# Moving the transposes of the gated activation to the border between the float32r and the bf16 products of gate/up

## The chip, the cores and the metric

The kernel runs on one core of a Trainium2 chip. The metric is the device time of one execution in microseconds. Five engines work side by side, each through its own list of instructions in order: TensorE (PE; PEld is its loading of weights), VectorE (DVE), ScalarE (ACT), GpSimd (POOL) and SyncE (SP), which issues most transfers. They hand work to each other by semaphores.

## The reference

One encoder block over 1024 tokens of width 1024: RMSNorm, one projection to q, k and v, differential attention beside dilated window attention, an output projection with a residual, RMSNorm, sixteen experts that each choose 128 tokens, a residual, and a final RMSNorm. The change lies in the experts:

```python
def expert_choice_ffn(h, w_router, w_gate, w_up, w_down):
    cap = EC_K * S // N_EXPERTS            # 128 tokens per expert
    aff = jax.nn.softmax((h @ w_router).astype(jnp.float32), axis=-1)
    g, idx = lax.top_k(aff.transpose(0, 2, 1), cap)
    ...
    def run_expert(args):
        wg, wu, wd, ie, ge = args
        xe = h[b_rows, ie]
        he = jax.nn.silu(xe @ wg) * (xe @ wu)
        return (he @ wd) * ge[..., None].astype(h.dtype)
```

## The kernel before, in words

An expert's hidden width of 2816 is worked in 11 slices of 256 columns. One slice of one expert is a **unit**; there are 16 x 11 = 176 of them, and the loop over them (L1487 to L1501) is where the kernel spends two thirds of its time.

Each float32 matrix is split in two. ScalarE writes the high part `wh` as float32r (L1324), VectorE subtracts it and writes the rest `wl` as bf16 (L1326). The text calls the first a **split** and the second a **subtraction**; each takes half a piece of weights (128 x 1024 numbers). A unit has three pieces: two of gate/up, one of down, so six splits and six subtractions. Of the activations there are a high part `xh` and a low part `xl`, both float32r.

For a unit i TensorE runs, in `gate_up`, sixteen float32r products with `wh` (L1354 with `xh`, L1355 with `xl`, by turns, k = 0 to 7) and then eight bf16 products with `wl` (L1363). ScalarE makes `sg`, the silu of the gate half (L1368), and VectorE multiplies it by the up half (L1369, the **gating product**). TensorE must turn `sg` before it can meet the down weights. That is done one unit late, in the middle of the products of unit i + 1: `middle` is called there, it emits the splits of the down weights of unit i, and `turn_gated` emits two transposes (L1375) and the splitting of their output into `eh` on ScalarE (L1381) and `el` on VectorE (L1382). Behind the bf16 products of unit i + 1 come the down products of unit i (`down`): four bf16 ones of `wl` with `eh` (L1392), then eight float32r ones, four with `eh` (L1395) and four with `el` (L1396). `sg`, `eh` and `el` have one buffer each.

The order on ScalarE and VectorE of all splits, subtractions, `sg`, `eh`, `el` and the gating product is the order in which the code emits them: `in_turn` ties each to the one before. On ScalarE a unit reads: eh, three splits, sg, three splits; the last two of these six are for the down weights. The scheduler of the tile framework places everything else, by its own costs. That holds for three things that come once per expert:

- **the end**: behind an expert's last down product ScalarE copies the output times its gate (ROW, L1454, two halves) and GpSimd adds it to the result in memory;
- **the pick**: in the unit behind s = 3 VectorE makes a one-hot matrix (L1226), TensorE takes eight small products with it (P, L1232), and VectorE reduces their output to token numbers and gates (L1234 to L1238), with which GpSimd fetches the next expert's rows;
- **the turned rows**: behind the unit of s = 8 TensorE turns these rows with eight transposes (L1297), and ScalarE and VectorE split them into the next `xh` and `xl` (L96).

`issue_behind(a, b)` only orders a behind b on their engine; it waits for nothing. In `gate_up` it ties the first product of k = 3 behind the last transpose (L1359), so the transposes stand after k = TG = 2. While the first expert runs, a search for the sixteen thresholds (L1174 to L1186) shares VectorE with it.

Of the kernel before, what the change touches and what calls it, by code (L numbers as in the profile page):

```python
# [49 lines left out]
PK, PT = 3, 8  # L50
PK0, PT0 = 6, 9
SB, XB = 1, 2
TG = 2
OHN = lambda e: 8
HIB, LOB = 8, 10
STQ = lambda t: 2
# [26 lines left out]
def tile_hybrid_encoder_block(ctx, tc, x, norm1_g, w_in, lam_v, subln_g, w_out, rel_bias, hot,  # L83
# [14 lines left out]
    def issue_behind(later, earlier):  # L98

        tc.add_manual_dep(later.ins, earlier.ins.name,  # L100
                          mybir.DependencyInfo(mybir.DependencyClass.NoSync, mybir.DependencyReason.DATA),
                          reason="issue_behind")
# [56 lines left out]
    def top(t):  # L159

        n = len(t.shape) - 1
        return t.bitcast(BF)[(slice(None),) * n + (slice(1, None, 2),)]
# [1142 lines left out]
    def in_turn(ins):  # L1305

        eng = str(ins.ins.engine)
        if eng in tails:
            issue_behind(ins, tails[eng])
        tails[eng] = ins  # L1310
        return ins
# [36 lines left out]
    def gate_up(xt, wt, middle):  # L1348
        _, _, xh, xl = xt
        pg = ps_g.tile([128, 2, FS], F32, name="pg")  # L1350
        cut = lambda k: [v(k % 4 * 512, 512) for v in wt[k // 4]]
        for k in range(KD):
            wh = cut(k)[0]
            hh = nc.tensor.matmul(pg, xh[:, k, :], wh, start=(k == 0), stop=False)  # L1354
            mm_ = nc.tensor.matmul(pg, xl[:, k, :], wh, start=False, stop=False)  # L1355
            if k == TG:
                last_mm[0] = mm_
                middle()
            if k == TG + 1 and turned_g:  # L1359
                issue_behind(hh, turned_g.pop())  # L1360

        for k in range(KD):
            low = nc.tensor.matmul(pg, top(xh)[:, k, :], cut(k)[1], start=False, stop=(k == KD - 1))  # L1363
            if k == 0:
                issue_behind(low, mm_)
        last_mm[0] = low
        sg = sm.tile([128, FS], F32, name="sg", bufs=SB)
        in_turn(nc.scalar.activation(sg, pg[:, 0, :], AF.Silu))  # L1368
        in_turn(nc.vector.tensor_mul(sg, sg, pg[:, 1, :]))  # L1369
        return sg  # L1370
# [88 lines left out]
    last_mm, last_hi, turned_g = [None], [None], []  # L1459
# [17 lines left out]
    def middle(i):  # L1477
        next(later, None)
        if i >= 0:
            split_piece(i, 2)  # L1480
            sgs[i] = turn_gated(sgs[i])
        if i + 2 < len(units):
            split_piece(i + 2, 0)
            if (i + 2, 1) not in split:
                split_half(i + 2, 1, 0)

    for i, (e, s) in enumerate(units):  # L1487
        load_pieces()
        wt = [parts(i, 0), parts(i, 1)]
        sgs[i] = gate_up(prep[e], wt, lambda: middle(i - 1))  # L1490
        if i + 1 < len(units):
            split_piece(i + 1, 1)
        next(later, None)
        if s == (PK if e else PK0) and e + 1 < n_experts:
            prep[e + 1] = pick(e + 1, slot_all[0][:, :, e + 1:e + 2])
        if s == (PT if e else PT0) and e + 1 < n_experts:
            prep[e + 1] = turn3(*prep[e + 1], after=last_mm[0])
        if i > 0:
            close(i - 1)
        if done_p[0] == len(pieces) and last is None and (s > 1 or n_experts == 1):  # L1500
            last = final_load()  # L1501
# [82 lines left out]
```

## Time and profile before

| | us |
|---|---|
| median of three runs | 2269.86 (2263.57 to 2271.57) |
| profiled execution | 2268.57 |
| its span | 2266.8 |
| TensorE busy | 2168.2 (96%) |
| VectorE busy | 1891.6 (83%) |
| ScalarE busy | 1600.3 (71%) |

The span runs from the first to the last instruction; the time of the execution has 1.8 us more around it. Busy times overlap, since the engines work side by side. In the chain of work that ended last TensorE has 84% of the span, VectorE 6%, transfers 5%. By lines, TensorE's products of gate/up (L1354, L1355, L1363) make 41% of it.

### The profile page before, as it was taken

What the parts mean: (1) busy time and instruction counts of PE and PEld (TensorE: products, weight loads), DVE (VectorE), ACT (ScalarE), POOL (GpSimd) and SP (SyncE); (2) the same over time, 40 slices, a digit from 0 to 9 for tenths busy, and PEclk for the clock granted to TensorE, in tenths of its full rate; (3) what the DMA queues carried; (4) which work ended last, traced back from release to release, by engine and by line L of the source; (5) the groups of instructions that cost most, each with busy time, mean ns of one, the idle gap of its engine ahead of it and who ended that gap; (6) DMA issues with size and microseconds to landing.
All of it is one profiled execution on the core that took longest, in us unless ns stands there. A gap on an engine that the chain in (4) does not pass through costs nothing.

```text
span 2266.8 us, 31806 instructions
## 1 busy us (share of the span) xinstructions
PE 2168.2 (96%) x11051; PEld 1604.7 (71%) x11171; DVE 1891.6 (83%) x2874; ACT 1600.3 (71%) x2431; POOL 223.6 (10%) x264
## 2 busy tenths in 40 slices
PE   8999998989996999999999999999999999999995
PEld 7899897767774666676666666666667667666663
DVE  5466774677877999999899999999999999999996
ACT  5576773556743677777777777787777777777785
POOL 1000100345533000000000000000000000000000
PEclk9999999999997999999999999999999999999998
DMA  5767656588568799999999999999999999999983
GB/s 185 233 179 209 182 164 171 154 200 224 177 232 267 275 360 392 374 385 390 367 401 374 377 386 375 406 373 377 388 371 397 374 390 385 374 388 381 388 344 129
DMA packets 172749, 708.25 MB, mean 312 GB/s; under 512 B 19690, under 2 KB 54634, under 8 KB 106658
## 3 DMA queue, kind: packets, MB, share of 16 engines
q1 hardware_dynamic: 160452, 670.46, 80.2%
q0 software_dynamic: 7184, 25.69, 4.0%
q10 hardware_dynamic: 4952, 10.05, 1.3%
q8 instruction: 88, 1.44, 0.3%
q14 instruction: 73, 0.60, 0.1%
HBM read 649.89 MB, written 57.75 MB: 312 GB/s over the span
## 4 chain that ended last, share of the span: by engine, by line
PE 84%; DVE 6%; DMA 5%; issue 2%; ACT 2%; SPq 0%; POOL 0%; POOLq 0%; ACTq 0%; DVEq 0%
PE pg L1354 14%; PE pg L1355 14%; PE pg L1363 13%; PE pm L154 10%; PE py L1396 7%; PE py L1395 7%; PE py L1392 6%; PE av L154 4%; PE ps L154 3%; PE pt L157 3%; PE px L1375 2%; PE py L154 1%; DVE wl L1326 1%; DMA xt<-xa_d 1%; DMA w<-q_d 1%
## 5 line engine op out<-in xcount | busy, mean ns | idle before, releaser
L1326 DVE TENSOR_TENSOR wl<-w,wh 128x1024 bf16<-128x1024 f32 (+1 forms) x1062 | 1237.9, 1217 | 74.9 <-ACT wh L1324 71.5
L1324 ACT ACTIVATE wh<-w 128x1024 fp32r<-128x1024 f32 (+1 forms) x1070 | 1041.6, 1041 | 8.9 <-DVE up L1088 5.4
L1354 PE MATMUL pg<-wh,xh 128*128 128x512 f32 x1408 | 570.7, 405 | 0.0
L1355 PE MATMUL pg<-wh,xl 128*128 128x512 f32 x1408 | 553.9, 393 | 1.3 <-DVE xl L96 1.3
L1363 PE MATMUL pg<-wl,xh 128*128 128x512 bf16 x1313 | 316.5, 380 | 6.3
L1395 PE MATMUL py<-wh,eh 128*128 128x512 f32 x704 | 310.7, 441 | 0.0
L1354 PEld LDWEIGHTS pg<-wh,xh 128*128 128x128 f32 x1408 | 265.5, 189 | 56.5 <-issue 2.1
L1355 PEld LDWEIGHTS pg<-wh,xl 128*128 128x128 f32 x1408 | 266.1, 189 | 53.9 <-DVE xl L96 2.0
L1396 PE MATMUL py<-wh,el 128*128 128x512 f32 x704 | 278.3, 395 | 0.0
L1363 PEld LDWEIGHTS <-xh 128*128 128x128 bf16 x1408 | 123.6, 98 | 170.0 <-issue 45.0
L1381 ACT ACTIVATE eh<-px 128x256 fp32r<-128x256 f32 x176 | 67.5, 384 | 166.0 <-PE px L1375 166.0
L1392 PE MATMUL py<-wl,eh 128*128 128x512 bf16 x701 | 180.4, 379 | 1.0 <-ACT eh L1381 0.9
L1368 ACT ACTIVATE sg<-pg 128x256 f32<-128x256 f32 x176 | 67.5, 384 | 137.6 <-PE pg L1363 137.6
L1395 PEld LDWEIGHTS py<-wh,eh 128*128 128x128 f32 x704 | 132.5, 188 | 44.3
L1396 PEld LDWEIGHTS py<-wh,el 128*128 128x128 f32 x704 | 132.5, 188 | 28.7 <-issue 0.4
L154 PE MATMUL pm<-hT,wh 128*128 128x512 f32 x464 | 146.6, 396 | 0.1
L1392 PEld LDWEIGHTS <-eh 128*128 128x128 bf16 x704 | 68.8, 98 | 80.4 <-ACT eh L1381 1.2
L1455 POOL DMA_INDIRECT x_d<-row,idx x15 | 24.1, 1607 | 933.7 <-ACT row L1454 870.3
L154 PE MATMUL pm<-wh,hT 128*128 128x256 f32 x512 | 102.4, 290 | 0.1
L154 PEld LDWEIGHTS pm<-hT,wh 128*128 128x128 f32 x464 | 83.9, 188 | 15.8 <-DVE ee L361 0.5
L418 ACT ACTIVATE e<-e,nm 128x1024 f32<-128x1024 f32 x64 | 73.5, 1148 | 29.3 <-DVE nm L416 22.8
L96 DVE TENSOR_TENSOR pl<-pt,ph 128x512 fp32r<-128x512 f32 x96 | 65.3, 684 | 33.0 <-ACT ph L96 33.0
(303 smaller groups left out, 2884.4 us busy)
## 6 DMA issues: line engine op xcount, KB each, us to landing
w<-in_w_moe_dram SPq DMA_DIRECT2D x514, 1024.0 KB, 7.3
w<-in_w_moe_dram SPq DMA_DIRECT2D x56, 256.0 KB, 4.2
wraw<-in_w_in_dram SPq DMA_DIRECT2D x48, 256.0 KB, 4.1
v_d<-ee SPq DMA_DIRECT2D x16, 512.0 KB, 4.0
q_d<-ee SPq DMA_DIRECT2D x16, 512.0 KB, 3.8
k_d<-ee SPq DMA_DIRECT2D x16, 512.0 KB, 3.4
k<-k_d SPq DMA_DIRECT2D x16, 512.0 KB, 6.0
xt<-in_x_dram SPq DMA_DIRECT2D x8, 512.0 KB, 6.9
```

Source lines behind the costliest of these rows:

```text
L154: return pin(nc.tensor.matmul(*args, **kw))
L157: return pin(nc.tensor.transpose(*args, **kw))
L418: nc.scalar.activation(e, e, AF.Exp, bias=nm, scale=-1.0, accum_out=l)
L1324: hi = nc.scalar.activation(wh[:, cs], src, AF.Copy)
L1326: sub = eng.tensor_sub(wl[:, cs], src, r32(wh)[:, cs])
L1354: hh = nc.tensor.matmul(pg, xh[:, k, :], wh, start=(k == 0), stop=False)
L1355: mm_ = nc.tensor.matmul(pg, xl[:, k, :], wh, start=False, stop=False)
L1363: low = nc.tensor.matmul(pg, top(xh)[:, k, :], cut(k)[1], start=False, stop=(k == KD - 1))
L1368: in_turn(nc.scalar.activation(sg, pg[:, 0, :], AF.Silu))
L1392: low.append(lambda j=j, c=c, ns=ns, n=n: nc.tensor.matmul(py[:, ns], top(eh)[:, j, :], wl(c, 512), start=(s == 0 and j == 0), stop=False))
L1395: nc.tensor.matmul(py[:, ns], eh[:, j, :], wh(c, 512), start=False, stop=False),
L1396: nc.tensor.matmul(py[:, ns], el[:, j, :], wh(c, 512), start=False, stop=(s == NS - 1 and j == 1))))
```

## The change

`TG` becomes 7. So `middle` is called behind the last float32r product of a unit instead of behind that of k = 2, and the transposes are ordered behind that product. The order that tied the product of k = 3 behind the transposes goes, and the first bf16 product is tied behind them instead.

```diff
-TG = 2
+TG = 7
 ...
             if k == TG:
                 last_mm[0] = mm_
                 middle()
-            if k == TG + 1 and turned_g:
-                issue_behind(hh, turned_g.pop())
 
         for k in range(KD):
             low = nc.tensor.matmul(pg, top(xh)[:, k, :], cut(k)[1], start=False, stop=(k == KD - 1))
             if k == 0:
                 issue_behind(low, mm_)
+                if turned_g:
+                    issue_behind(low, turned_g.pop())
         last_mm[0] = low
```

Two lines go in `gate_up`, so its bf16 products are on L1361 in the changed file; the other lines spoken of keep their numbers. The instructions are the same ones. Their order changes at four places.

On TensorE, in an ordinary unit, the transposes of `sg` (px<-ident,sg) stood between float32r products before:

```order
L1354 MATMUL pg<-wh,xh 128x512
L1355 MATMUL pg<-wh,xl 128x512
L1375 MATMUL px<-ident,sg 128x128 x2
L1354 MATMUL pg<-wh,xh 128x512
L1355 MATMUL pg<-wh,xl 128x512
```

and now:

```order
L1354 MATMUL pg<-wh,xh 128x512
L1355 MATMUL pg<-wh,xl 128x512
L1375 MATMUL px<-ident,sg 128x128 x2
L1361 LDWEIGHTS xh
L1361 MATMUL pg<-wl,xh 128x512
```

They moved past ten float32r products, to right ahead of the eight bf16 ones.

On TensorE, at the pick, the last of the eight products with the one-hot matrix `oh` stood ahead of the last float32r product:

```order
L1232 LDWEIGHTS oh
L1232 MATMUL pr<-aux,oh 128x5
L1355 MATMUL pg<-wh,xl 128x512
L1363 LDWEIGHTS xh
L1363 MATMUL pg<-wl,xh 128x512
```

and now, for eleven of the experts (py is the down output of the expert at work):

```order
L1232 LDWEIGHTS oh
L1232 MATMUL pr<-aux,oh 128x5
L1361 LDWEIGHTS xh
L1361 MATMUL pg<-wl,xh 128x512
L1392 LDWEIGHTS eh
L1392 MATMUL py_19250<-wl,eh 128x512
L1392 LDWEIGHTS eh
L1392 MATMUL py_19250<-wl,eh 128x512
L1354 MATMUL pg<-wh,xh 128x512
L1392 LDWEIGHTS eh
L1392 MATMUL py_19250<-wl,eh 128x512
```

The eight small products moved behind the seventh bf16 product, and one float32r product of the next unit stands among the down products. VectorE's own order at this place is unchanged: gating product, subtraction, one-hot, subtraction, the three reductions, subtraction, el.

On ScalarE, at the end of an expert, the two ROW copies (row<-py) stood together behind the fourth split:

```order
L1381 ACTIVATE eh<-px 128x256
L1324 ACTIVATE wh<-w 128x1024 x3
L1368 ACTIVATE sg<-pg 128x256
L1324 ACTIVATE wh<-w 128x1024
L1454 ACTIVATE row<-py_18363,gate 128x512 x2
L1324 ACTIVATE wh<-w 128x1024 x2
L1381 ACTIVATE eh<-px 128x256
```

and now, for twelve of fifteen experts:

```order
L1381 ACTIVATE eh<-px 128x256
L1324 ACTIVATE wh<-w 128x1024 x2
L1454 ACTIVATE row<-py_18363,gate 128x512
L1324 ACTIVATE wh<-w 128x1024
L1368 ACTIVATE sg<-pg 128x256
L1324 ACTIVATE wh<-w 128x1024
L1454 ACTIVATE row<-py_18363,gate 128x512
L1324 ACTIVATE wh<-w 128x1024 x2
L1381 ACTIVATE eh<-px 128x256
```

The first copy moved ahead of a split and of sg. For the first three experts both copies now stand behind the fifth split, where they stood behind the sixth. The fourth place, where rows are turned, changes likewise for eleven experts: TensorE's eight transposes are parted into four ahead of the bf16 down products and four behind them, and the copies on ScalarE and VectorE stand apart, the first right behind eh and el, the second behind two splits.

## Rows read from the trace of the kernel before

**Rows 1.** Windows: stretch, its us, busy us (count) per engine, granted clock, DMA share, GB/s.
```profile
743.00:803.00 60.00, 53.72 (x245) 35.04 (x249) 59.94 (x118) 38.77 (x49) 0.00 (x0) 1.00 0.87 307
1300.00:1400.00 100.00, 99.60 (x460) 69.10 (x465) 92.55 (x101) 77.66 (x99) 2.83 (x2) 1.00 0.98 387
```

**Rows 2.** Timeline of TensorE, an ordinary unit: start us, duration us, engine, line, operation, xcount.
```profile
1601.25 0.40 PE L1354 MATMUL pg<-wh,xh 128*128 128x512 f32 x1
...
1602.64 0.38 PE L1375 MATMUL px<-ident,sg 128*128 128x128 f32 x2
...
1603.09 0.39 PE L1355 MATMUL pg<-wh,xl 128*128 128x512 f32 x1
...
1604.93 0.39 PE L1355 MATMUL pg<-wh,xl 128*128 128x512 f32 x1
1605.39 1.67 PE L1363 MATMUL pg<-wl,xh 128*128 128x512 bf16 x7
1606.90 1.03 PE L1392 MATMUL py<-wl,eh 128*128 128x512 bf16 x4
...
1609.63 0.40 PE L1354 MATMUL pg<-wh,xh 128*128 128x512 f32 x1
```

**Rows 3.** Timeline of TensorE where an expert's rows are turned.
```profile
1559.90 0.38 PE L1375 MATMUL px<-ident,sg 128*128 128x128 f32 x2
...
1564.16 1.04 PE L1297 MATMUL px<-ident,row 128*128 128x128 f32 x8
1565.03 1.03 PE L1392 MATMUL py<-wl,eh 128*128 128x512 bf16 x4
1569.15 0.38 PE L1375 MATMUL px<-ident,sg 128*128 128x128 f32 x2
```

**Rows 4.** Timeline of ScalarE, the same place.
```profile
1560.32 0.38 ACT L1381 ACTIVATE eh<-px 128x256 fp32r<-128x256 f32 x1 [1.10 <-PE px L1375]
1560.60 2.00 ACT L1324 ACTIVATE wh<-w 128x1024 fp32r<-128x1024 f32 x2
1564.80 1.08 ACT L96 ACTIVATE xh<-px 128x512 fp32r<-128x512 f32 x2 [2.20 <-PE px L1297]
```

**Rows 5.** Timeline of VectorE, the same place.
```profile
1560.76 0.42 DVE L1382 TENSOR_TENSOR el<-px,eh 128x256 fp32r<-128x256 f32 x1
1561.68 2.36 DVE L1326 TENSOR_TENSOR wl<-w,wh 128x1024 bf16<-128x1024 f32 x2 [0.49 <-ACT wh L1324]
1565.43 1.29 DVE L96 TENSOR_TENSOR xl<-px,xh 128x512 fp32r<-128x512 f32 x2 [1.39 <-ACT xh L96]
...
1571.74 0.42 DVE L1382 TENSOR_TENSOR el<-px,eh 128x256 fp32r<-128x256 f32 x1
```

**Rows 6.** Timeline of TensorE at a pick.
```profile
1526.13 0.38 PE L1375 MATMUL px<-ident,sg 128*128 128x128 f32 x2
...
1528.42 0.36 PE L1232 MATMUL pr<-aux,oh 128*128 128x5 bf16 x8
```

**Rows 7.** Timeline of VectorE at the same pick.
```profile
1528.82 0.16 DVE L1234 TENSOR_REDUCE num<-pr 128x1 f32<-128x2 f32 x1 [1.74 <-PE pr L1232]
...
1529.08 1.22 DVE L1326 TENSOR_TENSOR wl<-w,wh 128x1024 bf16<-128x1024 f32 x1
1530.21 0.42 DVE L1382 TENSOR_TENSOR el<-px,eh 128x256 fp32r<-128x256 f32 x1
```

**Rows 8.** Timeline of TensorE: an expert's last down product.
```profile
1499.39 0.40 PE L1396 MATMUL py<-wh,el 128*128 128x512 f32 x1
```

**Rows 9.** Timeline of ScalarE at the same end of an expert.
```profile
1499.82 1.27 ACT L1454 ACTIVATE row<-py,gate 128x512 f32<-128x512 f32 x2 [1.40 <-PE py L1396]
1500.98 2.01 ACT L1324 ACTIVATE wh<-w 128x1024 fp32r<-128x1024 f32 x2
1502.87 0.38 ACT L1381 ACTIVATE eh<-px 128x256 fp32r<-128x256 f32 x1
```

**Rows 10.** Timeline of VectorE at the same end of an expert.
```profile
1504.34 0.42 DVE L1382 TENSOR_TENSOR el<-px,eh 128x256 fp32r<-128x256 f32 x1
```

## The prediction

> **What bounds the kernel now.** I read the windows of the trace first, then one ordinary unit of the experts on TensorE, and then the three places in an expert where something other than the ordinary unit happens. The windows show where the limit is: of 100 us among the experts TensorE is busy 99.60, VectorE 92.55, ScalarE 77.66, at a granted clock of 1.00 [rows 1]. So TensorE sets the pace, and VectorE has only some 7% to spare. In the unit's timeline the reader is to see that products follow each other with no hole: 8.38 us from the first product of one unit (1601.25) to that of the next (1609.63) [rows 2]. A float32r product takes 0.230 (eight from 1603.09 to 1604.93), a bf16 one 0.216 (seven from 1605.39 to 1606.90), and from the start of the transposes to the second product behind them 0.45 pass, so the pair costs 0.22 in its old place [rows 2].
>
> **A clock for one unit.** Let t = 0 be the start of the two transposes, with the number of the unit whose gated activation they turn left out. ScalarE's eh starts at 0.42 and its next split at 0.70 [rows 3, 4]; el starts on VectorE at 0.86 and its first subtraction at 1.78, because that one waits for ScalarE's split, which stands 1.08 before it [rows 3 to 5]. From then on a subtraction follows each 1.13 (1529.08 to 1530.21) [rows 7], a split on ScalarE each 0.945 (two from 1500.98 to 1502.87) [rows 9]; el and the gating product take 0.34 (their 0.42 less the 0.09 by which a subtraction's 1.22 overlaps the next). VectorE's order is el, three subtractions, the gating product, three subtractions, el; the last two of these six, call them D1 and D2, make the low halves of the down weights that TensorE's bf16 down products read. Thus D2 starts at 1.78 + 3 x 1.13 + 0.34 + 2 x 1.13 = 7.77 and is done at 8.99.
>
> **What the change takes away.** The transposes leave the float32r products and stand before the bf16 ones. Four transposes and a bf16 product in a row are seen already, where an expert's rows are turned: eight transposes from 1564.16, the bf16 product at 1565.03, so 0.109 each and nothing added at the end [rows 3]; a pair costs 0.218. The old switch from float32r to bf16 takes 0.46 for two products (1604.93 to 1605.39) where 0.230 + 0.216 = 0.446 would do [rows 2]. The gain is about 0.016 a unit, 175 units, 3 us. Its bounds are nothing and 0.03 a unit, 5 us. The Trainium skill ("TensorE: Matmul & The Clock Gate", section "Step-by-step: what each phase is for") says that TensorE pulls a weight load ahead of running products, so that the order of kinds would not matter; by that rule the 3 us fall away and the sum below ends 3 us higher; the row's 0.46 against 0.446 says that it is nearly so.
>
> **What it moves.** Ten float32r products now run before the transposes instead of after them: eh and el come 10 x 0.230 = 2.30 us later, and TensorE's demand for them does not. Behind the transposes stand eight bf16 products (0.22 + 1.73 = 1.95), then the down products: the first two want eh and D1 at 1.95, the next two want D2 at 2.38, and the first product with el comes at 3.04. The unit ends at 4.68, the next transposes start at 8.36. Before, the same demands were 2.30 later: D2 at 4.68. In an ordinary unit D2 is done at 8.99 and wanted at 8.36 + 2.38 = 10.74: the slack falls from 4.05 to 1.75 us, and nothing waits. The deadline of the gating product, which the transposes read, becomes 2.30 us looser in exchange. So the question is which places make VectorE or ScalarE lose more than 1.75 us against TensorE. The trace has three of them per expert, visible as el's lateness, beyond 0.86, behind its transposes: at the end of an expert 3.34 - 0.86 = 2.48 (el at 1504.34; the transposes six products behind the last product of 1499.39, at 1501.00) [rows 8, 10]; where the next expert's tokens are picked 4.08 - 0.86 = 3.22 [rows 6, 7]; where its rows are turned 2.59 - 0.86 = 1.73 [rows 3, 5]. All three were covered by 4.05. Less 1.75 they leave 0.73 + 1.47 + 0 = 2.2 us per expert. Since phases and orders shift, I work each one out anew.
>
> **End of an expert.** The last product's output is read by two ROW copies on ScalarE (L1454), which start 0.43 behind that product's start and take 0.58 each [rows 8, 9]. In the new order the first stands earlier, behind only two splits, so ScalarE, free at 2.59, is held until 4.45 + 0.43 = 4.88; queued behind it are a split, sg, a split, the second ROW, D1's and D2's splits and eh. They start at 5.46, 6.40, 6.67, 7.61, 8.19, 9.14 and 10.08. VectorE follows: subtraction 6.54, gating product 7.67, subtraction 8.01, D1 9.27, D2 10.40, done at 11.62. TensorE wants D2 at 10.74: it waits about 0.9. Twelve experts have this order (the first three put the copies behind five splits, which costs nothing): 10.8 us.
>
> **The pick.** VectorE's reduction num waits for eight small products (P, L1232) and starts 0.40 behind the first of them, D2 another 0.26 later [rows 6, 7]. P stood between float32r products; now it stands before the eighth bf16 product, at 8.36 + 0.22 + 7 x 0.216 = 10.09. So num comes at 10.49, D2 at 10.75, done at 11.97. TensorE has left only P (up to 0.3), one bf16 product, two down products and one early float32r product of the next unit (0.22 + 0.43 + 0.23) and would want D2 at 11.27: it waits 0.7, eleven times, 7.7 us.
>
> **The turned rows.** The eight transposes are split in two fours, the second behind the down products. ScalarE's first copy starts 0.64 behind the first transpose (1564.80) and VectorE's 0.63 behind that [rows 3 to 5]: 2.59 and 3.22. Two splits, a copy, a split, sg and three splits follow, on VectorE 4.18, 5.31, copy 6.44, 7.05, gating 8.18, 8.52, D1 9.65, D2 10.78, done 12.00. The next transposes come at 9.24, so D2 is wanted at 11.62: 0.4, eleven times, 4.4 us. In the ordinary unit behind each place VectorE gains some 0.3 to 0.9 back and D2 is in time.
>
> **The start.** From 743 to 803 us the first expert shares VectorE with the search for the threshold, and VectorE is busy 59.94 of 60 [rows 1]. It does the same work in a slightly other order, so I take 0. Bounds: TensorE's 6 us of idleness there are the most that could be won, and 0.86 of waiting for el in seven units, 6 us, could be lost.
>
> **The sum.** 10.8 + 7.7 + 4.4 - 3 = 20 us on the profiled execution's 2268.57 (span 2266.8; 1.3 below the median of three, 2269.86): 2289. The waits are not in the trace of before; their ends are 0 (slack enough) and the whole lateness with no slack, 12 x 2.48 + 11 x (3.22 + 1.73) = 84 us. I stay near the subtraction of the slack, since its terms all have rows: 2.2 by the old lateness, 2.0 by the new schedule.
>
> **Rivals.**
> - The slack holds (0.14). If hand-overs are 0.5 us quicker than I took them or ROW's wait ends earlier, only the gain is left: 2268.57 - 3 = 2266, not slower. For it speaks that the other 140 units have 1.75 to spare; against it that two of three old latenesses exceed that. It decides at 1.75 us.
> - One or two of the three places stall (0.12): the pick alone gives 2273, pick and end 2284; I call it 2277. The pick's chain is the tightest, as P itself is late.
> - The start decides (0.04). TensorE idles 6 us of 60 there [rows 1], waiting for VectorE. Were the transposes the thing that waits, moving them back would win up to 6, and if the later stalls also fail, 2260. VectorE's 59.94 speaks against it.
> - It grows (0.08). A stall leaves a lateness that meets the next place, or the granted clock falls. From 743 to 803 TensorE was busy 53.72 of 60 and was still granted 1.00 [rows 1]. The skill (same page, "A second HAM failure mode: psum-queue depth-cycling") tells of short idle times between products that make the clock go up and down; no such fall is in that row. The price, one stall in eight followed by a unit at half clock: 4 x 8.4 = 34 more, 2323; by lateness alone 12 x 0.9 more, 2300. I take 2310.
>
> **How the numbers follow.** My forecast has 0.62 and, alone, spans 2279 to 2300 (each stall 0.3 us less or more: 34 x 0.3 = 10). The range for 8 in 10 takes in the partial case below and part of the growth above: 2270 to 2303. About 0.5%, 11 us, is what a measurement of this kernel can tell from no change. Slower, above 2281: most of my forecast (0.59), the growth (0.08), a little of the partial case (0.03), 0.70. Within: 0.26. Faster, below 2258.5: 0.04.
>
> **What would show it.** Right: a unit without a special place at 8.36, transposes followed at 0.22 by a bf16 product; ROW waiting some 2.3 us on ScalarE; a wait of TensorE for L1326 before the third down product (L1392), 34 times, 0.4 to 0.9 each; idle time of VectorE before el in ordinary units. Wrong: TensorE still at 99.6 of 100 among the experts, or waits for another releaser (eh, the gating product), or a granted clock below 1.00 there.

## The result, and the profile after

The changed kernel takes 2280.10 us (median of five executions, 2278.15 to 2281.28); the kernel before, run beside it, 2267.09 (2263.57 to 2271.57). The ratio is 1.0055, with a 95% interval from 1.0044 to 1.0067: slower by some 13 us, or half a percent.

The windows answer to [rows 1] (same stretches, same columns):

```profile
743.00:803.00 60.00, 55.16 (x279) 37.26 (x278) 58.90 (x117) 39.87 (x51) 0.00 (x0) 1.00 0.92 325
1300.00:1400.00 100.00, 98.68 (x460) 70.01 (x459) 91.15 (x100) 75.20 (x97) 3.36 (x2) 1.00 0.97 374
```

Among the experts TensorE fell from 99.60 to 98.68 of 100, at the same granted clock of 1.00, the upper level (2.4 GHz). It now waits. (The 0.40 that was missing from 100 before are no waits: that trace lacks the record of the first bf16 product in many units, which is why [rows 2] shows x7. So TensorE was hardly ever idle.) The view of what TensorE's products waited for, from 1000 us to 2200 us (total us, times, longest), was empty before and now has one line:

```profile
PE py L1392 <- DVE wl L1326: 14.9, 34, 0.7
```

The bf16 down products wait for a subtraction, 34 times: 12 ends of an expert, 11 picks, 11 turned rows. The loading of weights (PEld) waits too, for a split, 24 times, twice at each of the 12 ends:

```profile
PEld pg L1354 <- ACT wh L1324: 9.1, 24, 0.5
```

**An ordinary unit.** TensorE's timeline, which answers to [rows 2]:

```profile
1545.38 0.38 PE L1375 MATMUL px<-ident,sg 128*128 128x128 f32 x2
1545.60 1.89 PE L1361 MATMUL pg<-wl,xh 128*128 128x512 bf16 x8
1547.33 1.03 PE L1392 MATMUL py<-wl,eh 128*128 128x512 bf16 x4
...
1548.42 0.39 PE L1396 MATMUL py<-wh,el 128*128 128x512 f32 x1
...
1550.04 0.39 PE L1354 MATMUL pg<-wh,xh 128*128 128x512 f32 x1
...
1553.43 0.39 PE L1355 MATMUL pg<-wh,xl 128*128 128x512 f32 x1
1553.67 0.38 PE L1375 MATMUL px<-ident,sg 128*128 128x128 f32 x2
```

From transposes to transposes 8.29 us pass (8.29 and 8.33 by turns), where 8.38 did before. The seven steps from 1548.42 to 1550.04 are 0.231 each; the fifteen float32r steps of gate/up from 1550.04 to 1553.43 (a step is from the start of one product to that of the next) are only 0.226. Before, these took 0.230 to 0.232 [rows 2]. In the units of 8.33 the first seven steps of gate/up are still slow.

How much a unit gained shows best over many. Take the first product of the second expert, and that of the fifth expert's second unit, 34 units later; no stall lies between. TensorE's timeline of the kernel before:

```profile
838.12 0.40 PE L1354 MATMUL pg<-wh,xh 128*128 128x512 f32 x1
...
1126.58 0.40 PE L1354 MATMUL pg<-wh,xh 128*128 128x512 f32 x1
```

and of the changed one:

```profile
832.61 0.40 PE L1354 MATMUL pg<-wh,xh 128*128 128x512 f32 x1
...
1118.98 0.40 PE L1354 MATMUL pg<-wh,xh 128*128 128x512 f32 x1
```

288.46 against 286.37: 2.09 / 34 = 0.062 us a unit.

**The end of an expert**, which answers to [rows 8 to 10]. TensorE's timeline:

```profile
1493.41 0.38 PE L1375 MATMUL px<-ident,sg 128*128 128x128 f32 x2
...
1500.78 0.40 PE L1355 MATMUL pg<-wh,xl 128*128 128x512 f32 x1
1501.18 0.50 PE L1354 MATMUL pg<-wh,xh 128*128 128x512 f32 x1
...
1502.21 0.38 PE L1375 MATMUL px<-ident,sg 128*128 128x128 f32 x2
...
1505.10 0.59 PE L1392 MATMUL py<-wl,eh 128*128 128x512 bf16 x2 [0.35 <-DVE wl L1326]
```

ScalarE's, with the idle time before an instruction and its releaser in brackets:

```profile
1494.10 1.99 ACT L1324 ACTIVATE wh<-w 128x1024 fp32r<-128x1024 f32 x2
1498.28 0.69 ACT L1454 ACTIVATE row<-py,gate 128x512 f32<-128x512 f32 x1 [2.18 <-PE py L1396]
...
1499.81 0.37 ACT L1368 ACTIVATE sg<-pg 128x256 f32<-128x256 f32 x1
```

VectorE's:

```profile
1499.95 1.23 DVE L1326 TENSOR_TENSOR wl<-w,wh 128x1024 bf16<-128x1024 f32 x1 [2.40 <-ACT wh L1324]
```

ROW holds ScalarE 2.18 us with a split and sg queued behind it, and VectorE stands idle 2.40 behind that split. TensorE pays twice: in this unit float32r products are late (1500.78 to 1501.18 is 0.40 instead of 0.23; their weights come from late splits, which is the second line of waits above), and in the next the third bf16 down product waits for D2.

**The pick**, which answers to [rows 6, 7]. TensorE, then VectorE:

```profile
1527.70 0.38 PE L1375 MATMUL px<-ident,sg 128*128 128x128 f32 x2
...
1529.43 0.34 PE L1232 MATMUL pr<-aux,oh 128*128 128x5 bf16 x8
...
1531.35 0.59 PE L1392 MATMUL py<-wl,eh 128*128 128x512 bf16 x2 [0.67 <-DVE wl L1326]
```

```profile
1529.81 0.16 DVE L1234 TENSOR_REDUCE num<-pr 128x1 f32<-128x2 f32 x1 [1.44 <-PE pr L1232]
...
1530.08 1.22 DVE L1326 TENSOR_TENSOR wl<-w,wh 128x1024 bf16<-128x1024 f32 x1
```

VectorE idles 1.44 for P; D2 starts 0.27 after num and TensorE waits for it.

**The turned rows**, which answer to [rows 3 to 5]. TensorE, then ScalarE:

```profile
1562.00 0.38 PE L1375 MATMUL px<-ident,sg 128*128 128x128 f32 x2
...
1565.24 0.60 PE L1297 MATMUL px<-ident,row 128*128 128x128 f32 x4
...
1571.18 0.38 PE L1375 MATMUL px<-ident,sg 128*128 128x128 f32 x2
...
1574.04 0.59 PE L1392 MATMUL py<-wl,eh 128*128 128x512 bf16 x2 [0.32 <-DVE wl L1326]
```

```profile
1564.58 0.60 ACT L96 ACTIVATE xh<-px 128x512 fp32r<-128x512 f32 x1 [1.78 <-PE px L1297]
```

ScalarE idles 1.78 for the first four, and the wait for D2 comes one unit on.

**The account.** Read from the traces as above: the start of each unit's first product (L1354), in a kernel's trace less that in the trace of before. Its drift over the 34 units is the gain of a unit; what it rises by over a place, with that drift taken out, is the stall there (means of 12, 11 and 11 places from the fifth expert on). The rows below the first belong to the experiments.

| kernel | a unit | end | pick | rows |
|---|---|---|---|---|
| changed | -0.062 | +1.01 | +0.72 | +0.45 |
| ROW in old order | -0.062 | +0.01 | +0.70 | +0.45 |
| P in old order | -0.065 | +1.02 | -0.06 | +0.45 |
| rows in old order | -0.067 | +1.00 | +0.74 | +0.02 |
| all three | -0.062 | 0.00 | -0.07 | +0.02 |
| TG = 5, all three | -0.026 | -0.01 | -0.03 | -0.02 |
| TG = 3 | -0.005 | +1.57 (11 of 12) | -0.08 | +0.01 |
| TG = 5 | -0.025 | +0.96 | +0.30 | +0.49 |

For the changed kernel: stalls 12 x 1.01 + 11 x 0.72 + 11 x 0.45 = 25.0; gain 164 units x 0.062 = 10.1; the first expert, from its second unit to its end, 1.7 less (0.6 of which is the same gain; the next four kernels of the table show the same 1.7). Here the second unit is counted from its second L1354 product, 742.00 before and 738.21 now, because its first one stands among the products of the first unit. 25.0 - 10.1 - 1.7 = 13.2, and 13.0 was measured. The profiled spans differ by only 9.6, because that execution reached the second unit 3.8 us early. In the traces of the seven kernels below it in the table this arrival lies anywhere from 4.3 us early to 1.4 us late, also among those that have the transposes in the same place, so it is not put down to the change. The first three experts, whose ROW, P and rows got other orders, show no stall.

### The profile page after: what moved, and what is told of

Same layout as the page of the kernel before. It is cut to its first block, busy times and chain, and to the rows that moved or that the text cites. A ratio compares the mean times of both kernels' runs of the same rounds, so it can differ in the third digit from the quotient of the medians.

```text
span 2276.4 us, 31925 instructions
## 1 busy us (share of the span) xinstructions
PE 2173.6 (95%) x11171; PEld 1628.8 (72%) x11171; DVE 1893.7 (83%) x2874; ACT 1585.1 (70%) x2431; POOL 231.2 (10%) x264
## 3 DMA queue, kind: packets, MB, share of 16 engines
q8 instruction: 88, 1.44, 0.3%
## 4 chain that ended last, share of the span: by engine, by line
PE 79%; DVE 11%; ACT 4%; issue 3%; DMA 2%; POOL 0%; SPq 0%; ACTq 0%; POOLq 0%; DVEq 0%
PE pg L1355 12%; PE pg L1354 12%; PE pm L154 11%; PE pg L1361 11%; PE py L1396 6%; PE py L1395 6%; PE py L1392 6%; DVE wl L1326 6%; PE av L154 4%; PE ps L154 3%; PE pt L157 3%; ACT wh L1324 2%; PE py L154 2%; PE px L1375 1%; PE pl L1047 1%
## 5 line engine op out<-in xcount | busy, mean ns | idle before, releaser
L1326 DVE TENSOR_TENSOR wl<-w,wh 128x1024 bf16<-128x1024 f32 (+1 forms) x1062 | 1237.0, 1212 | 76.9 <-ACT wh L1324 75.8
L1354 PE MATMUL pg<-wh,xh 128*128 128x512 f32 x1408 | 556.5, 395 | 0.1
L1361 PE MATMUL pg<-wl,xh 128*128 128x512 bf16 x1408 | 335.0, 379 | 0.0
L1354 PEld LDWEIGHTS pg<-wh,xh 128*128 128x128 f32 x1408 | 264.8, 188 | 67.5 <-ACT wh L1324 9.6
L1361 PEld LDWEIGHTS <-xh 128*128 128x128 bf16 x1408 | 137.3, 98 | 125.8 <-issue 1.2
L1392 PE MATMUL py<-wl,eh 128*128 128x512 bf16 x704 | 187.2, 379 | 16.3 <-DVE wl L1326 15.3
L1392 PEld LDWEIGHTS <-eh 128*128 128x128 bf16 x704 | 67.9, 98 | 100.0 <-issue 28.7
L1455 POOL DMA_INDIRECT x_d<-row,idx x15 | 31.7, 2115 | 940.4 <-ACT row L1454 940.4
L154 PE MATMUL pm<-hT,wl 128*128 128x512 f32 x232 | 91.4, 395 | 0.4 <-DVE wl L334 0.4
```

The source lines that it names most:

```text
L154: return pin(nc.tensor.matmul(*args, **kw))
L1326: sub = eng.tensor_sub(wl[:, cs], src, r32(wh)[:, cs])
L1392: low.append(lambda j=j, c=c, ns=ns, n=n: nc.tensor.matmul(py[:, ns], top(eh)[:, j, :], wl(c, 512), start=(s == 0 and j == 0), stop=False))
```

## The experiments

**The three places, one by one and together.** Theory: each stall comes from what now stands at its own place. Rival: with 1.75 us of slack the place doesn't matter.

ROW chained behind the fourth split, as before:

```diff
-            nc.scalar.activation(ys[:, ns], py[:, ns], AF.Copy, scale=gate)
+            in_turn(nc.scalar.activation(ys[:, ns], py[:, ns], AF.Copy, scale=gate))
```

> The changed kernel, with the two ROW copies of ScalarE (L1454) chained behind the fourth split of their unit, as they stood before, at the end of every expert; the pick and the turned rows are left. Theory 'the places' (each of the three stalls comes from what stands at its own place, in the order that came with the change, now that the slack is 2.3 us smaller): the first ROW no longer holds ScalarE with a split and the silu behind it, both parts of this stall go (0.50 in the unit of the last down products, 0.52 in the next, 12 experts), 12 us less than the changed kernel: 2268. TensorE's wait for L1326 comes 22 times instead of 34, some 9 us in all. Rival 'the slack alone' (the copies cost ScalarE 1.16 us wherever they stand, and 1.75 us of slack is not enough for that): the wait moves but stays, 2277 to 2281, with 34 waits.

Measured: 2269.07 us, ratio to the kernel before 1.0013 (1.0002 to 1.0023). TensorE's waits, 1000 to 2200 us:

```profile
PE py L1392 <- DVE wl L1326: 10.6, 22, 0.7
```

Twelve waits are gone, and both halves of the stall.

P held ahead of the transposes of its unit:

```diff
-    first_gather = []
+    first_gather, picked = [], []
 ...
-            nc.tensor.matmul(p[:, :5], oh[:, c, :], aux[:, c, e, :], start=(c == 0), stop=(c == NT - 1))
+            picked[:] = [nc.tensor.matmul(p[:, :5], oh[:, c, :], aux[:, c, e, :], start=(c == 0), stop=(c == NT - 1))][e < 2:]
 ...
-            if last_mm[0] is not None:
-                issue_behind(tr, last_mm[0])
+            for b in [last_mm[0]] * (last_mm[0] is not None) + picked:
+                issue_behind(tr, b)
```

> The changed kernel, with the eight small products of the pick (P, L1232) held ahead of the transposes of their unit, so that they stand among the float32r products again; the rest is left. Theory 'the places': P comes 2 us earlier, num no longer holds VectorE, the stall of 0.75 goes at eleven picks, 8 us less than the changed kernel: 2272; waits for L1326 23 times, 6 us in all. Rival 'the slack alone': the one-hot tiles and P's own 0.29 still come too late for the second down weight's low half, TensorE waits in a place further on, 2278 to 2281.

P then stands right ahead of the transposes, behind the last float32r product and not ahead of it as in the kernel before. Measured: 2272.46, ratio 1.0021 (1.0010 to 1.0032). The waits:

```profile
PE py L1392 <- DVE wl L1326: 7.4, 23, 0.4
```

The eight transposes of the rows in one group, ahead of the down products, and their copies behind the fourth split:

```diff
                 if after is not None:
-                    issue_behind(tr, after)
+                    issue_behind(tr, after); last_mm[0] = tr
-            split_act(xh[:, kg * 4:kg * 4 + 4], xl[:, kg * 4:kg * 4 + 4], pt)
+            [in_turn(x) for x in split_act(xh[:, kg * 4:kg * 4 + 4], xl[:, kg * 4:kg * 4 + 4], pt) if after]
```

> The changed kernel, with the eight transposes of the next expert's rows (L1297) in one group ahead of the down products, and their copies (L96) behind the fourth split of the unit, as in the first three experts; the rest is left. Theory 'the places': no stall of 0.46 at eleven turned rows, 5 us less than the changed kernel: 2275; waits for L1326 23 times, some 11 us. Rival 'the slack alone': two copies of 0.54 each on ScalarE and 0.65 each on VectorE still have to fit in 1.75 us of slack, the wait stays, 2279 to 2281.

Measured: 2276.06, ratio 1.0039 (1.0025 to 1.0054). The waits:

```profile
PE py L1392 <- DVE wl L1326: 11.6, 23, 0.7
```

All three edits together:

> The three restorations together: ROW copies behind the fourth split, P ahead of the transposes, the eight transposes of the rows in one group with their copies behind the fourth split; the transposes of the gated activation stay where the change put them. Theory 'the places': all 25 us of stalls go and the gain of 0.06 a unit and of the start stays: 2255, 12 below the kernel before; TensorE waits for L1326 hardly at all from 1000 us on. Rival 'the slack alone': 2272 to 2281, not below the kernel before. A further possibility, that the start's 5.6 us were an accident of one execution: 2260.

Measured: 2256.28, ratio 0.9953 (0.9937 to 0.9969): 11.5 us below the kernel before, and the best version found. TensorE waits for nothing from 1000 us on; its window among the experts, to be held against [rows 1]:

```profile
1300.00:1400.00 100.00, 100.00 (x470) 71.51 (x469) 93.28 (x102) 77.44 (x99) 3.04 (x2) 1.00 1.00 388
```

Each of the four came within 1.3 us of its theory. The executions of one kernel scatter by more than that, so the account above is the firmer evidence: each edit takes its own stall to within 0.07 of zero and leaves the others. So the stalls are separate and add up, and the small slack is enough once the old orders stand. (Forecast as 1.75 us, it can be read from an ordinary unit of the changed kernel: D2 is done 0.67 behind the transposes, the third down product comes at 2.38, so 1.71.)

Why it is enough shows in el's lateness, the time from the start of the transposes to that of el. Before, it was 3.34 at the end, 4.09 at the pick and 2.60 at the rows (means of the same places); here it is 1.07, 1.81 and 0.92. At a pick, TensorE's timeline, then VectorE's:

```profile
1244.88 0.41 PE L1375 MATMUL px<-ident,sg 128*128 128x128 f32 x2
```

```profile
1246.70 0.42 DVE L1382 TENSOR_TENSOR el<-px,eh 128x256 fp32r<-128x256 f32 x1
```

**Does the slack matter at all?** TG = 3 and TG = 5 in the kernel before, with whatever orders come.

```diff
-TG = 2
+TG = 3
```

> TG = 3 in the kernel before: the transposes two float32r products later, the orders as they come: the first ROW behind two splits, as in the changed kernel; P behind the first bf16 product; the rows' transposes in one group. The clock of one unit gives 3.6 us of slack. Theory 'slack times place' (an order costs only what is left of it after the slack): nothing waits, a unit of 8.37, 2265 to 2267. Rival 'the order alone' (a ROW ahead of the silu or a P among the bf16 products stops TensorE whatever the slack): 12 x 1.0 + 11 x 0.5 more, 2284.

Measured: 2282.84, ratio 1.0049 (1.0031 to 1.0067). The theory that I favoured expected 2265 to 2267 and fell. The waits, then ScalarE, VectorE and TensorE at an end of an expert:

```profile
PE px L1375 <- DVE sg L1369: 16.3, 11, 1.5
```

```profile
1597.02 0.69 ACT L1454 ACTIVATE row<-py,gate 128x512 f32<-128x512 f32 x1 [4.04 <-PE py L1396]
```

```profile
1599.83 0.41 DVE L1369 TENSOR_TENSOR sg<-sg,pg 128x256 f32<-128x256 f32 x1
```

```profile
1600.30 0.44 PE L1375 MATMUL px<-ident,sg 128*128 128x128 f32 x2 [1.48 <-DVE sg L1369]
```

With TG = 3 the first ROW stands behind two splits, as in the changed kernel. ScalarE now waits 4.04 for it, and sg is behind it. D2 is in time, but the gating product isn't: the transposes wait. Slack at D2 is bought with the gating product's deadline, and a ROW ahead of sg costs at either end.

```diff
-TG = 2
+TG = 5
```

> TG = 5 in the kernel before, the orders as they come: the first ROW behind two splits, P behind five bf16 products, the rows' transposes in two fours, all as in the changed kernel or nearly; the transposes come 0.92 us earlier than there, so 2.7 us of slack instead of 1.75. Theory 'slack times place': the measured stalls of the changed kernel less 0.92 leave nothing at the rows and the pick and at most 0.1 at the end of an expert: 2262 to 2265. By the subtraction of the old latenesses from the slack (2.48, 3.22, 1.73 less 2.67) the pick alone would wait 0.55, 11 times: 2269. Rival 'the order alone': all three stalls, 25 us, 2288.

Measured: 2283.32, ratio 1.0057 (1.0040 to 1.0075); nearest to the rival, which expected 2288. The waits:

```profile
PE px L1375 <- DVE sg L1369: 8.1, 23, 0.4
PE py L1392 <- DVE wl L1326: 2.7, 11, 0.2
```

The stalls at the end and at the rows are nearly as large as with 1.75 us of slack (0.96 and 0.49 in the account), only the releaser changed; the one at the pick fell from 0.72 to 0.30.

**Where 0.062 a unit comes from.** First the transposes at TG = 5 with the three old orders.

```diff
-TG = 2
+TG = 5
 (and the edits of the three places)
```

> The transposes four float32r products ahead of the bf16 products (TG = 5 in the kernel before, tied behind the sixth pair), with the three old orders. Theory 'the run of float32r products': four products stand behind the break at 0.231 to 0.238 instead of 0.227, and the border costs its 0.02 again, so a unit of 8.35, 0.04 more than with the transposes at the border: 2256 + 7 = 2263, no waits for L1326. Rival 'the border': 8.37 as in the kernel before, as the pair is still within the float32r products: 2266.

Measured: 2260.85, ratio 0.9968 (0.9955 to 0.9980); it waits for nothing. A unit, from transposes to transposes:

```profile
1537.04 0.38 PE L1375 MATMUL px<-ident,sg 128*128 128x128 f32 x2
...
1545.38 0.38 PE L1375 MATMUL px<-ident,sg 128*128 128x128 f32 x2
```

8.34, by turns with 8.37: the 8.35 of the theory. A gain of 0.026 is there before the border is reached, so not all of the 0.062 is the border's.

Then a second pair of transposes at the old place, on top of the best version:

```diff
-            wh = cut(k)[0]
-            hh = nc.tensor.matmul(pg, xh[:, k, :], wh, start=(k == 0), stop=False)
+            wh, pt = cut(k)[0], ps_x.tile([128, 2, 128], F32, name="px") if k == 3 else None
+            hh = nc.tensor.matmul(pg, xh[:, k, :], wh, start=(k == 0), stop=False); extra(pt, hh, k and mm_)
 ...
+    def extra(pt, hh, mm_):
+        for j in range(2 if pt is not None else 0):
+            tr = nc.tensor.transpose(pt[:, j, :], ident, ident)
+            issue_behind(tr, mm_); issue_behind(hh, tr)
```

> The kernel with the three old orders and the transposes ahead of the bf16 products, and in every unit a second pair of 128-column transposes (of a constant, never read) at the old place, behind the third pair of float32r products: added work, 176 pairs. The question is why a unit became 0.063 shorter, and not 0.016. Theory 'the run of float32r products' (after each break a float32r product follows at some 0.231 and only after about 15 of them at 0.227; a pair in their midst starts that anew): the pair costs its own 0.217 and as much as the change gave, 0.05 to 0.06, so a unit of 8.58, 2256 + 176 x 0.27 = 2303, and the products behind the pair at 0.229 to 0.235. Rival 'the border' (all of the gain sits where float32r products change to bf16, and a pair costs 0.217 wherever it stands in float32r products): a unit of 8.53, 2256 + 176 x 0.217 = 2294, the products behind the pair at 0.227.

Measured: 2310.74, ratio 1.0173 (1.0155 to 1.0190), above both. TensorE's timeline in an ordinary unit (the pair is L1374), and its waits:

```profile
1565.64 0.39 PE L1354 MATMUL pg<-wh,xh 128*128 128x512 f32 x1
...
1567.00 0.38 PE L1374 MATMUL px<-ident 128*128 128x128 f32 x2
...
1567.45 0.40 PE L1355 MATMUL pg<-wh,xl 128*128 128x512 f32 x1
...
1569.31 0.40 PE L1355 MATMUL pg<-wh,xl 128*128 128x512 f32 x1
```

```profile
PE px L1374 <- DVE xl L96: 4.5, 13, 0.4
```

The six steps ahead of the pair are 0.227 each, the eight behind it 0.2325, where the theory had 0.229 to 0.235 and the rival 0.227: the run of float32r products is the theory that holds. The length of a unit alone would hardly decide: it is 8.56, 0.25 longer than the 8.31 of the best version, where the theory expected 8.58 and the rival 8.53. The time is 8 us above the theory. 4.5 of these are waits that I had not counted: the pair writes to the buffers that the rows' transposes use, and waits until xl has read them; the rest was not followed up.

What breaks a run? The same pair as two bf16 products of 128 columns, and as two float32r ones (one execution each):

```diff
-            tr = nc.tensor.transpose(pt[:, j, :], ident, ident)
+            tr = nc.tensor.matmul(pt[:, j, :], same, same, start=True, stop=True)
```

> As the kernel with the second pair, but the pair are two bf16 products of 128 columns (of a constant, never read). The question is what breaks a run of float32r products. Theory 'kind' (any product that is not float32r starts the slow stretch anew): the ten float32r products behind the pair follow each other at 0.229 to 0.235 again, as behind the transposes (0.2325). Rival 'transposes' (the transposes, being float32 work, do it): 0.227 behind the pair.

```diff
-            tr = nc.tensor.transpose(pt[:, j, :], ident, ident)
+            tr = nc.tensor.matmul(pt[:, j, :], xh[:, 0, :], xh[:, 1, :], start=True, stop=True)
```

> The same with two float32r products of 128 columns as the pair (xh with xh, never read). Theory 'kind': the run isn't broken, the products behind stay at 0.227. Rival 'any short product' (a change of length is enough): 0.229 to 0.235 behind it.

Measured: 2295.78 and 2305.49 beside 2265.70 of the kernel before; the times hold other waits too and are not compared. TensorE's timeline with the bf16 pair, then with the float32r pair:

```profile
1607.82 0.29 PE L1374 MATMUL px<-same 128*128 128x128 bf16 x2
...
1608.23 0.39 PE L1355 MATMUL pg<-wh,xl 128*128 128x512 f32 x1
...
1609.62 0.39 PE L1355 MATMUL pg<-wh,xl 128*128 128x512 f32 x1
```

```profile
1606.54 0.33 PE L1374 MATMUL px<-xh 128*128 128x128 f32 x2
...
1607.00 0.39 PE L1355 MATMUL pg<-wh,xl 128*128 128x512 f32 x1
...
1608.59 0.39 PE L1354 MATMUL pg<-wh,xh 128*128 128x512 f32 x1
```

Behind the bf16 pair six steps take 1.39, 0.232 each; behind the float32r pair seven take 1.59, 0.227 each. A change of kind starts the slow stretch anew, a short product of the same kind does not.

Put together, by the mean steps of 22 ordinary units in the trace of before and in that of the changed kernel: the eight steps behind the old place of the transposes took 0.034 less in all, the product right behind that place 0.007 less, the float32r down products 0.009 less, and the border 0.013 less. So about 0.05 of the 0.062 lies in the steps of float32r products, and the rest in the border.

## Why the prediction was right, and where it was not

The forecast was slower, at 2289, with 2279 to 2300 for itself; 2280.1 came, near the lower end. The prediction drew its line for "slower" at 2281, 0.5% over 2269.86; 2280.1 is just under it, and it is the ratio of 1.0055 to the kernel run beside it that shows the slowdown clear of noise. Step by step:

- **What bounds the kernel.** Right: TensorE sets the pace, and every stall reached the end.
- **What the change takes away** is the step that was mis-sized: "The gain is about 0.016 a unit, 175 units, 3 us", with 0.03 as its upper bound. It was 0.062, 10.8 us. I counted the switch alone (0.46 against 0.446), which was about right (0.013 measured), and took the steps of the products on either side as given. They aren't: a float32r product costs 0.231 for a while behind a break and 0.227 later, and in their old place the transposes were a second break in every unit. That is 7.8 us too little gain. The start took off another 1.1, and the stalls went the other way: 25.0 measured against 22.9 forecast. Together this makes the forecast 20 us over the kernel before into 13. The last 2 of the 8.9 us are rounding and the starting point, 2268.57 in the forecast and 2267.09 beside the changed kernel. That the time lay inside the range all the same is because this term is small beside the stalls.
- **What it moves.** The schedules hold, the subtraction of the slack doesn't. It said that latenesses of 2.48, 3.22 and 1.73 meet a slack of 1.75 and leave 2.2 us per expert; with all three old orders at the same slack nothing waits, and for TG = 5 it gave 2269 where 2283 came. The lateness was counted from the transposes, but ROW and P come at fixed places among TensorE's products; when the transposes move later by 2.3, that lateness shrinks as the slack does, from 3.34 to 1.07 and from 4.09 to 1.81 with the old orders. The stalls come from the new orders, which the subtraction knows nothing of. That it agreed with the schedules' 2.0 was chance.
- **End of an expert**, 0.9 forecast, 1.01 measured. ROW starts 4.87 behind the transposes (4.88 forecast), the third down product 11.69 (11.62). The split behind ROW was also late for TensorE's float32r products, which I had not seen: half of the loss is there (9.1 us of waits of weight loads in the 12 ends), and the wait at D2 is that much shorter.
- **The pick**, 0.7 forecast, 0.72 measured. P 1.73 behind the transposes (forecast 10.09 - 8.36 = 1.73), the third down product 3.65 (3.61).
- **The turned rows**, 0.4 forecast, 0.45 measured. The first copy at 2.58 (2.59), the third down product at 12.04 (12.00).
- **The start**, forecast 0: 1.7 less, 1.1 without the gain of a unit. Inside its bounds; its mechanism was not sought.
- **The rivals.** "The slack holds" and "one or two of the three places stall" fail on the 34 waits, "the start decides" on its size, "it grows" on the clock of 1.00 and on stalls that came at nearly the forecast size.
- **The signs.** An ordinary unit is 8.29 to 8.33, not 8.36; ROW waits 2.18 (2.3 forecast); the 34 waits came, by L1326 and at L1392, and last 0.3 to 0.7 (0.4 to 0.9 forecast).

The Trainium skill ("TensorE: Matmul & The Clock Gate", "Step-by-step: what each phase is for") puts products in a row one column per cycle apart, and with a fixed cost of issue on top gives 0.216 for 512 columns at the upper level of the clock. The bf16 row agrees (1545.60 to 1547.33, 0.216 each); the float32r rows are at 0.227 and 0.231, and the difference between these two is most of the gain. The prediction took from the pull-ahead of weight loads in the same section that the order of kinds would not matter. The section does not say that, and here it does matter: the same products in another order took 0.062 less a unit.

## What to carry to other kernels

Moving one instruction in a kernel whose order a scheduler fills in moves others; list these and price each, since here they cost 25 us while the move itself gained 12, and pinning three of them back turned a loss of 13 us into a gain of 11.5. A copy that waits for TensorE's last product belongs behind everything in its queue that TensorE will ask for sooner. Slack counted from a moving point is no measure of what a wait costs: draw up the schedule of the new order instead.

## What the runs showed of the hardware

- Behind a change of kind (from bf16 products or transposes) float32r products of 128x512 follow each other at about 0.231 us, and only later at 0.227. How much later differs: behind the bf16 down products 8 in the changed kernel's units of 8.29 and about 15 in those of 8.33; behind the bf16 pair 7; behind the second pair of transposes not within the 8 steps shown. A pair of 128-column transposes between them thus made a unit 0.25 longer, where its own time is 0.217. What in TensorE settles is open.
- Two float32r products of 128 columns do not start the slow stretch anew (0.227 behind them); two bf16 products do (0.232). Each was seen in one execution.
